# A hybrid decoder layer on one core: later due times for the values that come back from DRAM, and the gates' products in two parts

## The chip, the cores and the metric

The kernel runs on one core of a Trainium2 chip. The metric is the device time of one execution in microseconds (us), as the median of several runs; less is better. The engines that matter are TensorE (PE in the profile, with its weight loads apart as PEld), ScalarE (ACT), VectorE (DVE), GpSimd (POOL) and SyncE (SP), whose queue issues the DMAs.

## The reference: what is computed

One inference step of a decoder layer with width 2048, for 256 tokens of a new sequence and 8 × 8 tokens of running ones: 320 tokens in all, in float32.

```python
proj = jnp.einsum('btd,de->bte', x, w_in)
(ml_q, ml_k, ml_v, ml_i, ml_f, ml_o, hg_q, hg_f, hg_i, hg_g, gate_a, gate_b) = jnp.split(proj, offs, axis=-1)
...
ig = (ml_i + b_ig).transpose(0, 2, 1)
lf = jax.nn.log_sigmoid(ml_f + b_fg).transpose(0, 2, 1)
h, C, n, m = _mlstm(q, k, v, ig, lf, C0, n0, m0)       # 4 heads, key width 256, value width 512
...
o, S = _hgrn2(hq, jnp.log(f), 1.0 - f, hi, S0)         # 8 heads, key width 128, value width 256
...
merged = jax.nn.sigmoid(gate_a) * ya + jax.nn.sigmoid(gate_b) * yb
x1 = _layernorm(DEEPNORM_ALPHA * x + merged @ w_out, ln1_g, ln1_b)
y  = _layernorm(DEEPNORM_ALPHA * x1 + relu(x1 @ w_up)**2 @ w_down, ln2_g, ln2_b)
```

The outputs are y and the new states C, n, m and S of both groups of tokens. `ml_i` and `ml_f` are eight columns only, the input and forget gates of the four mLSTM heads; everything that decays in these heads is worked out from them.

## The kernel before, in words

**Tiles and units.** The weights of all the big products are cut into 304 tiles of 128 columns, in the order of `TILES`: for each of the four mLSTM heads four tiles of values (`mv`), two of keys (`mk`), two of queries (`mq`) and two of the merge gates; then for each of the eight HGRN heads merge gates, `hf`, `hq` and two `hi`; then the output gates, the branch projections, `w_out`, and the feed-forward part. A tile is sixteen steps over k, each with 128 rows of the weight and all 320 tokens. Each step is three matmuls, since a float32 number is held as a high and a low half: xh·wh, xl·wh and xh·wl. All of them are line 340, as the helper `mm` issues them. The first three tiles are interleaved over k, because x and the weights are still arriving (x comes in chunks of `FIRST_K`: one k at a time to 10, then two at a time).

**Weights.** Half a tile is a unit, 128×1024 floats, 512 KB. It is loaded into one of three raw buffers (`wr<-wt`), ScalarE writes its high half (`wh<-wr`, line 334, called from `prep`), VectorE the low half (`wl<-wr,wh`, line 504, in `low_half`), and then the load of the third unit after it is issued (`reload`). Hence the two splitting engines have a unit of weights to do every 24 matmuls, and do all else between.

**The order of the work** comes from a planner that runs while the program is written (`Sched`, lines 145 to 240). It keeps a clock for every engine, `s.t`. The main loop, `run_main`, writes the matmuls of a step, adds 147 ns each to the clock of PE, and then calls `pump`. That lets chains (generators, by priority) put their own next instructions on the engines, where the planner's times allow it: a request `("act", cost, fn)` is written at once if it would be ready soon; `wait(e)` holds the chain until the planned time `e.t`; `acq` and `rel` take and give buffers and banks. Each engine runs its instructions in the order written; semaphores keep the data right. So a planned time moves no data: it decides behind what an instruction stands in its engine's queue.

**What the change touches.**

- `gates`, line 762, is called by `run_main` ahead of step (0, 10), that is, tile 0, k = 10. It multiplies the sixteen chunks of x with the eight gate columns (in all sixteen products of 32 output rows, four row strips side by side in one bank), adds 2500 ns to PE's clock, and starts two chains. `rows` (line 798) copies the bank, sums the strips (two products with the constant `sel`, `bank<-f,cst`), and makes everything that decays: Abs, Exp and Ln on ScalarE, the rest on VectorE; its results are stored to DRAM (`scr<-f`) and each head reads its rows of it back, broadcast to all partitions (`f2a<-scr`, in `m_E`). `lb` (line 772) does the bounds of the HGRN gates.
- `m_V`, line 973. The values of an mLSTM head are transposed by 32×32 blocks on VectorE and stored to DRAM in four DMAs (`rows_to`, `vtD<-f`); `rows_from` (line 1014) reads them back as 128×1024 (`ra<-vtD`), waits in the plan for 5000 ns after the issue, and then splits them: ScalarE `ra<-ra` 128×1024 (line 334), VectorE `ra<-ra` (line 1808, in `split`).
- `h_i`, line 1571, the same for the values of an HGRN head (`sD`, `f2r<-sD`, 128×512).

**What stands around it.** In each mLSTM head `m_KW` (line 1077) multiplies the keys with the decay (line 1087), transposes them by blocks (line 1097), splits them (lines 334 and 1100), sums them (lines 1109 to 1111), and stacks the halves of the sample tokens' keys: `f<-f2a` on ScalarE and line 1058 on VectorE, followed by two transposes on TensorE (line 1122). This happens twice, so there are two pairs of transposes in a head. `m_CP` stores keys (`kD<-ra`), `turned` (lines 1303 to 1325) stores the heads' outputs (`hT<-f`, with its own transposes, line 1320, and copies `f<-bank` of 128×64).

**Queues.** All these DMAs, and the weights', are issued by SP in the order written (line 343); the profile calls that SPq.

Of the kernel before, what the change touches and what calls it, by code (L numbers as in the profile page):

```python
# [21 lines left out]
KT = 16  # L22
# [212 lines left out]
def wait(*evs):  # L235
    return ("wait", evs)


def acq(pool, n=1):
    return ("acq", pool, n)  # L240


def rel(pool, item):
    return ("rel", pool, item)


def post(ev):
    return ("set", ev)
# [47 lines left out]
class Program:  # L296
# [216 lines left out]
    def run_main(self):  # L513
        s = self.s
        todo, step = {}, []
        for n, (i, k) in enumerate(STEPS):
            t = TILES[i]
            u = i + FIRST * (k // 8) if i < FIRST else 2 * i + k // 8
            if n == 0:
                self.first()  # L520
            elif (i, k) == (0, 10):
                self.gates()
            if k == 0:
                self.before(i, t)
                pool = self.sbank if i == FIRST - 1 else self.mbank
                s.until(lambda: pool.free)
                pool.free.sort(key=lambda x: x[0])
                at, b = pool.free.pop(0)
                mh, ml, evs = self.moving(t)
                todo[i] = pool, b, b[:, :mh.shape[2]], mh, ml, evs  # L530
                s.t["pe"] = max(s.t["pe"], at)
                if t[0] == "up":
                    self.up_old[t[1:3]] = self.old[0]
            pool, b, o, mh, ml, evs = todo[i]
            if t[0] == "up" and not self.old[k]:
                o, mh, ml = b[:, :TOK], self.xh, self.xl
                s.t["pe"] = max(s.t["pe"], self.u_at[k])
            if i < FIRST:
                s.t["pe"] = max(s.t["pe"], self.x_at[k])
            while self.prep(u not in self.unit):  # L540
                pass
            assert u in self.unit, (u, self.next_prep)
            (hi, lo), at = self.unit[u]
            if evs is not None:
                s.until(lambda: evs[k].t is not None)
                at = max(at, evs[k].t + LAT)
            kk = slice(128 * (k % 8), 128 * (k % 8) + 128)
            step.append((i, t, u, b, o, hi[:, kk], lo[:, kk], mh, ml))
            if i < FIRST - 1:
                continue  # L550

            s.t["pe"] = max(s.t["pe"], at)
            for n in range(3):
                if i < FIRST and k == KT - 1:
                    break
                for _, _, _, _, o, wh, wl, mh, ml in step:
                    self.mm(o, wl if n == 2 else wh, (ml if n == 1 else mh)[:, k, :], start=n + k == 0, stop=n == 2 and k == KT - 1)
                s.t["pe"] += 147.0 * len(step)
                if n < 2 and i < FIRST:
                    s.pump(s.t["pe"])  # L560
            if t[0] == "up" and self.want[k] is not None:
                self.want[k].t, self.want[k] = s.t["pe"], None
            for i, t, u, b, o, wh, wl, mh, ml in step:
                if i < FIRST and k == KT - 1:
                    for n in range(3):
                        self.mm(o, wl if n == 2 else wh, (ml if n == 1 else mh)[:, k, :], start=False, stop=n == 2)
                    s.t["pe"] += 441.0
                if k % 8 == 7:
                    self.give(u)
                if k == KT - 1:  # L570
                    del todo[i]
                    s.spawn(self.evac(t, b), 0)
                if i < FIRST - 1:
                    s.pump(s.t["pe"])
            step = []
            s.pump(s.t["pe"])
        self.carve_o()
        self.main_end.t = s.t["pe"]
        s.until(lambda: not s.chains)
# [179 lines left out]
        for x, name, sl in ((self.n0_in, "n0", np.s_[:]), (self.lmask, "lmask", np.s_[:])):  # L759
            yield ("sp", 620, lambda: self.dma(x, d[name][sl]))  # L760

    def gates(self):

        s, b = self.s, self.gbank
        for k in range(KT):
            x = k % 4
            self.mm(b[32 * x:32 * x + 32, :TOK], self.gw[:, k, :], self.xs[:, k, :], start=k < 4, stop=k >= KT - 4)
        s.t["pe"] += 2500.0
        s.spawn(self.rows(b), 1)
        s.spawn(self.lb(), 2)  # L770

    def lb(self):

# [199 lines left out]
    def m_V(self, h):  # L973
        m = self.mh[h]
        if h:
            yield wait(self.mh[h - 1]["Vt"])
        yield wait(*m["v"])
        vr = m["vr"]
        yield from self.rows_to(vr[:, 0:1024], self.vtD[h])
        yield wait(m["Vs"])  # L980
        yield rel(self.vr, vr)
        vhl = yield acq(self.vhl)
        m["vhl"] = vhl
        yield from self.rows_from(self.vtD[h], vhl[:, 0], vhl[:, 1])
        yield post(m["Vt"])

    def m_Vs(self, h):
# [23 lines left out]
        e.t = t + 5000.0  # L1011
        yield wait(e)

    def rows_from(self, of, hi, lo):

        x = lo.bitcast(F32)
        t = yield ("sp", 620, lambda: self.dma(x.rearrange("p (n k) -> p n k", k=128), of.rearrange("j (i p) k -> p (j i) k", p=128)))
        e = Ev()
        e.t = t + 5000.0
        yield wait(e)  # L1020
        yield from self.split(x, hi, lo, hi.shape[1])

# [548 lines left out]
    def h_i(self, h):  # L1571
        m = self.hh[h]
        if h:
            yield wait(self.hh[h - 1]["I"])
        yield wait(*m["i"])
        yield self.mdone()
        yield from self.rows_to(m["iv"][:, 0:512], self.sD[h])
        it = yield acq(self.it)
        m["it"] = it
        yield from self.rows_from(self.sD[h], *it)  # L1580
        yield post(m["I"])

    def h_vs(self, h):
# [656 lines left out]
```

## Time and profile before

| | us |
|---|---|
| median of three runs | 2285.47 |
| lowest, highest | 2284.47, 2285.81 |
| the profiled execution | 2287.0 |
| its span in the profile | 2285.2 |

The mean granted clock of TensorE in the profiled execution is 0.998. In the profile's groups a line such as `L334 ACT ACTIVATE wh<-wr 128x1024 ... x431` is one kind of instruction: line 334 of the kernel, on ScalarE, from tile `wr` to tile `wh`, 431 times. In the timeline a row gives start, duration, engine, line, operation, tiles and shapes, how many of them in a row, and in brackets how long the engine had been idle ahead of it and what ended this idle time. A matmul's duration (0.31 us) is its time through the array; a new one starts every 0.147 us.

### The profile page before, as it was taken

Reading aid. Unit: us, or ns where it says so; the run is one execution under the profiler, and the core shown is the slowest. Engines: PE = TensorE matmul, PEld = TensorE weight load, DVE = VectorE, ACT = ScalarE, POOL = GpSimd, SP = SyncE. Lnnn points to the kernel's source line nnn. Section 1 sums busy time; section 2 is a strip of 40 time slices with the busy share of each in tenths; the row PEclk is TensorE's granted clock in tenths of the full one; section 3 lists DMA queues with packets and bytes.
Section 4 is the critical chain, followed back from the end, with each engine's and each line's share of the span. In section 5 each row is a group of like instructions: output and inputs, shape, how many; then the busy total and the mean of one; then the engine's idle time right before and its main releaser. Section 6 shows DMA issues by size and latency. Waiting matters only on the chain.

```text
span 2285.2 us, 39088 instructions
## 1 busy us (share of the span) xinstructions
PE 2270.6 (99%) x15546; PEld 2232.6 (98%) x15546; DVE 1422.2 (62%) x2490; ACT 1010.8 (44%) x1574; POOL 12.3 (1%) x42
## 2 busy tenths in 40 slices
PE   9999999999999999999999999999999999999998
PEld 9989899999999999999999999999999999999998
DVE  6667667888888876555555769444444444444555
ACT  5444445555555565444433447433433343334434
POOL 0000000000000000000000000000000000000000
PEclk9999999999999999999999999999999999999999
DMA  7898886666677655544555644444444444444555
GB/s 240 322 292 281 295 270 224 205 221 208 212 226 233 204 180 178 175 171 172 175 174 191 205 157 148 152 153 148 148 150 154 148 148 151 153 148 148 193 185 185
DMA packets 253536, 441.28 MB, mean 193 GB/s; under 512 B 106908, under 2 KB 149028, under 8 KB 252328
## 3 DMA queue, kind: packets, MB, share of 16 engines
q1 hardware_dynamic: 250664, 432.48, 56.8%
q0 software_dynamic: 2688, 6.29, 0.9%
q8 instruction: 122, 2.00, 0.4%
q14 instruction: 62, 0.51, 0.1%
HBM read 380.45 MB, written 58.24 MB: 192 GB/s over the span
## 4 chain that ended last, share of the span: by engine, by line
PE 92%; DMA 3%; DVE 1%; ACT 1%; SPq 1%; issue 0%; ACTq 0%; DVEq 0%
PE bank L340 92%; DMA wr<-wt 1%; SPq L343 1%; DVE wl L504 1%; DMA ra<-vtD 0%; ACT f3m L334 0%; ACT wh L334 0%; DMA f<-xT 0%; DMA f2a<-scr 0%; DMA scr<-f 0%; DMA hT<-f 0%; DMA rx<-wt 0%; ACT oC L334 0%; ACT f L334 0%; ACT ra L334 0%
## 5 line engine op out<-in xcount | busy, mean ns | idle before, releaser
L340 PE MATMUL bank<-xh,wh 128*128 128x320 f32 x2408 | 759.7, 317 | 0.0
L340 PE MATMUL bank<-xh,wl 128*128 128x320 f32 x2408 | 743.9, 310 | 0.8 <-DVE wl L504 0.8
L340 PE MATMUL bank<-xl,wh 128*128 128x320 f32 x2408 | 740.9, 309 | 0.0
L334 ACT ACTIVATE wh<-wr 128x1024 fp32r<-128x1024 f32 (+1 forms) x431 | 452.3, 1049 | 614.1 <-PE bank L340 575.8
L504 DVE TENSOR_TENSOR wl<-wr,wh 128x1024 fp32r<-128x1024 f32 x423 | 516.6, 1221 | 304.3 <-ACT wh L334 301.6
L340 PEld LDWEIGHTS bank<-xh,wh 128*128 128x128 f32 x2408 | 453.1, 188 | 6.4 <-issue 3.9
L340 PEld LDWEIGHTS bank<-xl,wh 128*128 128x128 f32 x2408 | 453.1, 188 | 2.6
L340 PEld LDWEIGHTS bank<-xh,wl 128*128 128x128 f32 x2408 | 453.5, 189 | 1.3 <-DVE wl L504 1.3
L334 ACT ACTIVATE bb<-wr 128x1024 fp32r<-128x1024 f32 x179 | 189.6, 1060 | 356.0 <-PE bank L340 342.3
L504 DVE TENSOR_TENSOR bb<-wr,bb 128x1024 fp32r<-128x1024 f32 x179 | 219.0, 1224 | 163.1 <-ACT bb L334 163.1
L340 PE MATMUL bank<-xh,bb 128*128 128x320 f32 (+1 forms) x1280 | 284.1, 309 | 0.0
L340 PE MATMUL bank<-ra,bb 128*128 128x320 f32 x1264 | 283.3, 308 | 0.0
L340 PE MATMUL bank<-rxb,bb 128*128 128x320 f32 x1112 | 255.0, 309 | 0.0
L340 PE MATMUL bank<-ra,wh 128*128 128x320 f32 x892 | 248.8, 308 | 0.0
L340 PEld LDWEIGHTS bank<-xh,bb 128*128 128x128 f32 x1280 | 214.6, 188 | 0.0
L340 PEld LDWEIGHTS bank<-ra,bb 128*128 128x128 f32 x1264 | 210.6, 188 | 0.2
L340 PE MATMUL bank<-xl,bb 128*128 128x320 f32 (+1 forms) x640 | 197.5, 309 | 0.0
L340 PEld LDWEIGHTS bank<-rxb,bb 128*128 128x128 f32 x1112 | 188.4, 188 | 0.2
L340 PE MATMUL bank<-rxb,wl 128*128 128x320 f32 x596 | 183.7, 308 | 0.0
L340 PE MATMUL bank<-rxb,wh 128*128 128x320 f32 x596 | 183.7, 308 | 0.0
L340 PEld LDWEIGHTS bank<-ra,wh 128*128 128x128 f32 x892 | 161.4, 188 | 0.0
L340 PEld LDWEIGHTS bank<-xl,bb 128*128 128x128 f32 x640 | 120.2, 188 | 0.0
(325 smaller groups left out, 2132.9 us busy)
## 6 DMA issues: line engine op xcount, KB each, us to landing
wr<-wt SPq DMA_DIRECT2D x602, 512.0 KB
rx<-C SPq DMA_DIRECT2D x34, 256.0 KB
Cs<-rx SPq DMA_DIRECT2D x34, 256.0 KB
f<-C SPq DMA_DIRECT2D x30, 256.0 KB
Cs<-f SPq DMA_DIRECT2D x30, 256.0 KB
f<-xT SPq DMA_DIRECT2D x26, 160.0 KB
vD<-ra SPq DMA_DIRECT2D x4, 1024.0 KB
f<-S SPq DMA_DIRECT2D x8, 512.0 KB
```

The source lines that it names most:

```text
L334: return self.nc.scalar.activation(out, in_, func, **kw)
L340: self.nc.tensor.matmul(*a, **kw)
L343: self.nc.sync.dma_start(out, in_)
L504: self.V().tensor_tensor(lo, raw, hi.bitcast(F32), ALU.subtract)
```

## The change

The gates' products are written in two parts, k = 0 to 11 ahead of step (0, 10) and k = 12 to 15 ahead of step (0, 12), and cost the plan 78 ns each (1248 in all) and not 2500; `rows` and `lb` start behind the second part. The wait between the issue of a readback and its split is 10000 ns for the mLSTM values and 7000 ns for the HGRN values, where both had 5000. Each engine gets as many instructions as before; the order in which they are written is another. From line 772 on the changed kernel's lines have a number one higher (the split is line 1809, the transposes 1123).

```diff
-            elif (i, k) == (0, 10):
-                self.gates()
+            elif i == 0 and k in (10, 12):
+                self.gates(*((0, 12) if k == 10 else (12, KT)))
...
-    def gates(self):
+    def gates(self, k0, k1):
...
-        for k in range(KT):
+        for k in range(k0, k1):
             x = k % 4
             self.mm(b[32 * x:32 * x + 32, :TOK], self.gw[:, k, :], self.xs[:, k, :], start=k < 4, stop=k >= KT - 4)
-        s.t["pe"] += 2500.0
-        s.spawn(self.rows(b), 1)
-        s.spawn(self.lb(), 2)
+        s.t["pe"] += 78.0 * (k1 - k0)
+        if k1 == KT:
+            s.spawn(self.rows(b), 1)
+            s.spawn(self.lb(), 2)
...
-        yield from self.rows_from(self.vtD[h], vhl[:, 0], vhl[:, 1])
+        yield from self.rows_from(self.vtD[h], vhl[:, 0], vhl[:, 1], 10000.0)
...
-    def rows_from(self, of, hi, lo):
+    def rows_from(self, of, hi, lo, ahead):
...
-        e.t = t + 5000.0
+        e.t = t + ahead
...
-        yield from self.rows_from(self.sD[h], *it)
+        yield from self.rows_from(self.sD[h], *it, 7000.0)
```

## The prediction

> **What bounds the kernel now.** I read the page first, then the waits of TensorE, then the timeline of each engine at every wait found.
>
> ```profile
> PE 2270.6 (99%) x15546; PEld 2232.6 (98%) x15546; DVE 1422.2 (62%) x2490; ACT 1010.8 (44%) x1574; POOL 12.3 (1%) x42
> ...
> PE 92%; DMA 3%; DVE 1%; ACT 1%; SPq 1%; issue 0%; ACTq 0%; DVEq 0%
> ...
> 824.78 1436.54 PE bank L340 x9787
> ...
> PE bank L1122 <- DVE f2a L1058: 2.5, 1, 2.5
> PE bank L1122 <- DVE f L1058: 1.9, 1, 1.9
> PE bank L340 <- POOL ones L666: 1.0, 1, 1.0
> PE bank L340 <- DVE wl L504: 0.8, 2, 0.5
> PE bank L340 <- DMA f<-xT: 0.6, 1, 0.6
> PE bank L340 <- ACT f2r L334: 0.4, 1, 0.4
> ```
>
> TensorE is busy for 99% of the span. The chain's long piece gives 1436.54 / 9787 = 0.147 us per matmul, and no number of matmuls changes. So all that the change can win is the waits. Without the first one, of POOL, which it doesn't touch, they are 2.5 + 1.9 + 0.8 + 0.6 + 0.4 = 6.2 us. The 1.9 us one was followed by slow matmuls:
>
> ```profile
> 233.13 0.31 PE L340 MATMUL bank<-xh,wl 128*128 128x320 f32 x1
> 235.38 0.33 PE L1122 MATMUL bank<-cst,f 128*128 128x128 f32 x1 [1.95 <-DVE f L1058]
> ...
> 236.53 0.62 PE L340 MATMUL bank<-xh,wh 128*128 128x320 f32 x1
> ...
> 239.61 0.41 PE L340 MATMUL bank<-xh,wl 128*128 128x320 f32 x1
> ...
> 200.00:300.00 100.00, 98.05 (x663) 92.79 (x662) 70.28 (x141) 43.92 (x83) 0.00 (x0) 0.98 0.88 282
> ```
>
> From 236.53 to 239.61 eleven matmuls take 0.28 us each where 0.147 is usual: 1.5 us more, in the one stretch of 100 us whose granted clock is 0.98 and not 1.00. The ceiling of the gain is thus about 6.2 + 1.5, with some 0.2 us of slow restart after each wait near 9 us: 0.4% of the span. I call 0.2% (4.57 us) the least that a measurement of this kernel tells from no change.
>
> The sum below is made against the profiled run, 2287.0 us with a span of 2285.2. It is 1.5 us above the median of the runs, 2285.47, so I take 1.5 off at the end. Shifts are those of TensorE after against before; plus is later.
>
> **1. The gates' products in two parts.**
>
> ```profile
> 19.18 1.52 PE L340 MATMUL bank<-f 128*32 128x320 f32 x16
> 21.25 0.73 PE L340 MATMUL bank<-f 128*32 128x320 f32 x4 [0.55 <-DMA f<-xT]
> ...
> 28.29 1.04 ACT L334 ACTIVATE wh<-wr 128x1024 fp32r<-128x1024 f32 x1
> 29.90 0.47 ACT L334 ACTIVATE f<-f 4x320 f32<-4x320 f32 x1 [0.57 <-DVE f L823]
> 30.96 1.39 ACT L334 ACTIVATE f<-bank 128x256 f32<-128x256 f32 x6 [0.59 <-PE bank L340]
> ...
> 31.65 0.31 PE L340 MATMUL bank<-xh,wh 128*128 128x320 f32 x1
> ```
>
> The 0.55 us wait for the last chunk of x goes: its transfer lands while 18 other matmuls (2.6 us) run. Against it stands a second change from full to 32-row products and back. No row prices one alone: the rows leave 21.25 to 31.65 without a gap that could be it, so I bound it by 0 and by two pitches, 0.3, and take 0.15, between ends that are near each other. Gain 0.4.
>
> But the chain of the gates (ScalarE's Abs and Exp, two weight splits between them) starts 18 matmuls later too. Those pieces now fall at 30 to 31.5 us, right ahead of the six copies that empty the first three tiles' banks. Before, the copies start at 30.96, take 0.23 each, and the fourth tile's first matmul follows at 31.65. In the changed order one 1.04 us split and one 0.47 us step come just before them, and bank 0's second copy is the fourth and not the second of the six: 2 × 0.23 = 0.46, and of the 1.5 us ahead I count a third, since ScalarE sat idle for 0.59 and 0.57 there. Shift at 32 us: about +0.9, the gain above included; from −0.4 (all hidden) to +1.4.
>
> **2. Head 0.** There the readback's halves move 39 matmuls back.
>
> ```profile
> 60.37 0.35 DVE L928 TENSOR_SCALAR f<-f2a,misc 128x256 f32<-128x256 f32 x1 [3.87 <-DMA f2a<-scr]
> ...
> 61.72 1.23 DVE L1808 TENSOR_TENSOR ra<-ra 128x1024 fp32r<-128x1024 f32 x1
> ...
> 63.67 1.22 DVE L504 TENSOR_TENSOR wl<-wr,wh 128x1024 fp32r<-128x1024 f32 x1
> ...
> 64.95 0.42 PE L340 MATMUL bank<-xh,wl 128*128 128x320 f32 x1 [0.28 <-DVE wl L504]
> ...
> 70.32 0.33 PE L1122 MATMUL bank<-cst,f 128*128 128x128 f32 x1
> ```
>
> The gates' rows come back from DRAM at 60.3; their chain begins 2.6 us later and may regain 0.7 to 1.5 of that where ScalarE stood idle (0.57, 0.59), so I take 61.4 to 62.2. The weights' low half (63.67) no longer has the readback's 1.23 us in front of it, so it ends near where it did. From the rows to the transposes (70.32) it was 10.0 us; without the readback's 1.23 in between, of which I count 0.5 to 1, it is 9 to 9.5: transposes at 70.9 to 71.7 with the nearer ends paired. Shift: +1.0 (+0.2 to +1.8), no longer hidden by anything: VectorE's chain is what ends last here.
>
> **3. Head 1, the longest wait.**
>
> ```profile
> 147.87 1.06 ACT L334 ACTIVATE ra<-ra 128x1024 fp32r<-128x1024 f32 x1 [3.59 <-DMA ra<-vtD]
> 148.83 0.42 ACT L334 ACTIVATE f<-bank 128x320 f32<-128x320 f32 x1
> ...
> 152.80 1.06 ACT L334 ACTIVATE wh<-wr 128x1024 fp32r<-128x1024 f32 x1 [2.10 <-DMA wr<-wt]
> 153.76 0.29 ACT L334 ACTIVATE f<-f2a 128x128 fp32r<-128x128 f32 x1
> ...
> 148.96 1.23 DVE L1808 TENSOR_TENSOR ra<-ra 128x1024 fp32r<-128x1024 f32 x1 [2.74 <-ACT ra L334]
> ...
> 155.03 0.28 DVE L1058 TENSOR_TENSOR f<-f2a,f 128x128 fp32r<-128x128 f32 x1
> ...
> 152.28 0.33 PE L1122 MATMUL bank<-cst,f2a 128*128 128x128 f32 x1 [2.54 <-DVE f2a L1058]
> ...
> 156.09 0.27 PE L1122 MATMUL bank<-cst,f 128*128 128x128 f32 x1
> ...
> 147.88 0.44 SPq L343 DMA_DIRECT2D wr<-wt  x1
> ```
>
> Before, the halves wait until 147.87 for the readback, and the key's small pieces queue behind them on ScalarE and VectorE: so the first transposes wait 2.54 us. The change puts the halves 36 and 39 matmuls back, behind those pieces; the first transposes are then ready at about 149.3, and this wait goes.
>
> What is late next is the second pair, 24 matmuls on (156.09). In the new order its piece f<-f2a stands on ScalarE behind a weight split and then the readback's half, and on VectorE behind L504 and L1808. The weight split waits for wr, which SP issues at 147.88, at its place in a queue that the change does not reorder up to there; so it still starts at 152.80. Then 153.86 + 1.06 = 154.9 for the half, + 1.23 = 156.2 for L1808, + 0.28 and a start for L1058: transposes at about 156.5. TensorE, there by 153.3, waits 3.2 us. Shift behind it: +0.4 by these absolute times, up to +1.4 if SP carries the +1.0 of head 0; −2.1 if the weights land 2.5 us sooner. Taken: +0.7. The wait moves by 4 us and is not shorter.
>
> A page speaks for the change: the Trainium skill, "DMA: Bandwidth & Descriptors", section "Rules for kernel authors", has it that a DMA is issued early and its semaphore awaited late, so that its fixed cost lies beside work. By that rule alone the 2.54 us go; the rows agree for the first pair, and 152.80 speaks against it for the second.
>
> **4. Heads 2 and 3.**
>
> ```profile
> 231.74 1.06 ACT L334 ACTIVATE ra<-ra 128x1024 fp32r<-128x1024 f32 x1 [3.46 <-DMA ra<-vtD]
> ...
> 233.64 0.22 ACT L334 ACTIVATE f<-bank 128x64 f32<-128x64 f32 x1 [0.41 <-DMA hT<-f]
> ...
> 234.71 0.30 ACT L334 ACTIVATE f<-f2a 128x128 fp32r<-128x128 f32 x1
> ...
> 315.78 1.06 ACT L334 ACTIVATE ra<-ra 128x1024 fp32r<-128x1024 f32 x1 [4.08 <-DMA ra<-vtD]
> ...
> 319.75 0.42 PE L340 MATMUL bank<-xh,wl 128*128 128x320 f32 x1 [0.50 <-DVE wl L504]
> ```
>
> Head 2: the half no longer stands before f<-f2a, but the copies f<-bank still do, and one of them waits for a store hT to land at 233.6. Behind it come 0.22 + 0.42 + 0.30 on ScalarE and 0.28 on VectorE: transposes at 234.8, not 235.38. That is −0.6; but the second pair, 36 matmuls on, now has the half and one weight split in front of it on both engines, and I count +0.6 there (one 1.06 us piece that isn't quite covered). The bounds of head 2 are −3.5 (wait and slow matmuls go) and +2.3 (half and split halves, 1.06 + 1.23, uncovered). Head 3: the half goes 30 matmuls back, and the wl that was 0.50 late is ready before it is asked: −0.5, from −0.7 to +0.5.
>
> On the 1.5 us of slow matmuls: the Trainium skill, "TensorE: Matmul & The Clock Gate", section "What's actually happening", says that the clock is halved after about one idle window of 3.4 us, free-running. This trace has it after 1.95 us and not after 2.54; by the page it is chance, and the 3.2 us of head 1 would cost by my estimate up to half a window, 1.7 us. I leave the 1.5 in both.
>
> **5. The HGRN heads.** The wait of 7 us moves the 128x512 halves 12 to 45 matmuls back in five heads; in three they come 12 to 42 earlier, as the planner has shifted what lies around them. In the new order 18 to 78 matmuls (2.6 us and more) stand between each and its first reader. The one wait there (0.4) may go or move: 0, from −0.5 to +1.5. From 824.78 on the chain is TensorE alone, and the order is the same.
>
> **Queues.** No engine gets an instruction more. SP keeps the order of the vtD stores, readbacks and weight loads in heads 0 and 1; in head 2 one hT store, whose copy waits for the landing at 233.6 or the one before it, comes ahead of a weight load. That load goes out some 3 us later, but it is for the third unit after the one at hand (a unit is 24 matmuls, 24 × 0.147 = 3.5 us), so I cost it at nothing. POOL's order is untouched.
>
> **Sum.** +0.7 after head 1; −0.6 and +0.6 in head 2; −0.5 in head 3; 0 in the HGRN heads: +0.2, so about 2287.2 profiled, **2285.7** as a median.
>
> **Rivals.**
> - **A, the waits really go.** Weights land in time in head 1 and the stores in head 2: 2.5 + 1.9 + 0.5 + 0.6 (gates), 1.5 of slow matmuls, less 1.0 to 2.0 of head 0: −5 to −6, 2279.5 to 2280.5. For it: the first pair is free by 149.3. Against it: the waits of 2.10 for wr and 0.41 for hT, which have nothing to do with the halves. This is also what the rule of awaiting late gives.
> - **B, slower: the late half blocks the second pair in every head.** Each loses 1.06 + 1.23 = 2.3 us where TensorE was on time before. It decides where the half is issued behind a weight split whose transfer lands less than 3.5 us before the pair is due. Three heads, less the first pair's gain in head 1, plus the 1.0 of head 0: 3 × 2.3 − 2.5 + 1.0 = +5.4, and +6.9 with 1.5 of slow matmuls in a second place: 2290.9 to 2292.4. For it: head 1 above. Against it: in head 2 the half stands 30 matmuls (4.4 us) ahead of the pair that it could block.
> - **C, it does nothing to the time:** the halves are issued later, but wait for the same landings (147.87, 231.74, 315.78 on ScalarE): ±0.5 us.
>
> **How the numbers follow.** Forecast, waits that move: 0.45, within 0.2%. A: 0.25, nearly all faster by over 0.2%. B: 0.25, slower by over 0.2%. C: 0.05, within. So faster 0.25, same 0.50, slower 0.25. The range leaves out about the far half of A and of B: 2280 to 2291.5.
>
> **What would show it.** Right: no wait at 149 us, one of about 3 us before an L1122 at 153 to 157; ScalarE's `wh` near 152.8 still waiting for wr; the fourth tile's start at 32.3 to 32.8; transposes of head 0 at 71. Wrong: TensorE without a wait of over 1 us between 100 and 330 (A), or three of over 2 us (B); or another granted clock in a stretch after 330 us.

## The result, and the profile after

| | before | after |
|---|---|---|
| median of 18 runs each, us | 2287.99 | 2291.31 |
| lowest, highest, us | 2284.47, 2289.63 | 2283.78, 2294.97 |
| span of the profiled execution, us | 2285.2 | 2289.5 |

The ratio is 1.0015, with a 95% interval from 1.0009 to 1.0021: 2 to 5 us slower, 3.4 in the middle. It is less than the 0.2% that the prediction called the least that can be told from no change; with eighteen runs of each it can just be told. The forecast time, 2285.7, was reckoned from three runs of the kernel before with a median of 2285.47; in these eighteen it takes 2287.99. So 2.5 of the 5.6 us between 2285.7 and 2291.31 are not the change's. The time lies just inside the forecast range, 2280 to 2291.5.

The waits of TensorE in the profile after (what was waited for, us in total, times, longest):

```profile
PE bank L1123 <- DVE f L1059: 8.6, 3, 3.3
PE bank L340 <- ACT f L334: 1.0, 1, 1.0
PE bank L340 <- POOL ones L666: 1.0, 1, 1.0
PE bank L1123 <- DVE f2a L1059: 0.9, 1, 0.9
```

Without POOL's they are 8.6 + 1.0 + 0.9 = 10.5 us, where before they were 6.2. The difference, 4.3, is that of the two spans (2289.5 − 2285.2 = 4.3). Of the old waits that the change could touch one is left, that of the first pair of transposes in head 2 (1.95 us at 235.38 before, 2.69 at 237.38 now). The others are gone, and there are four new ones. In the timeline (start, duration, engine, line; in brackets the idle time and what ended it):

```profile
32.16 0.41 PE L340 MATMUL bank<-xh,wh 128*128 128x320 f32 x1 [1.01 <-ACT f L334]
...
156.63 0.33 PE L1123 MATMUL bank<-cst,f 128*128 128x128 f32 x1 [3.33 <-DVE f L1059]
...
237.38 0.33 PE L1123 MATMUL bank<-cst,f 128*128 128x128 f32 x1 [2.69 <-DVE f L1059]
...
321.08 0.33 PE L1123 MATMUL bank<-cst,f2a 128*128 128x128 f32 x1 [0.88 <-DVE f2a L1059]
...
328.94 0.33 PE L1123 MATMUL bank<-cst,f 128*128 128x128 f32 x1 [2.55 <-DVE f L1059]
```

The longest is the one that the prediction gave for head 1 (156.5, 3.2 us). The queue of ScalarE and then of VectorE there, in the timeline of the changed kernel:

```profile
152.92 1.06 ACT L334 ACTIVATE wh<-wr 128x1024 fp32r<-128x1024 f32 x1 [5.63 <-DMA wr<-wt]
153.88 1.04 ACT L334 ACTIVATE ra<-ra 128x1024 fp32r<-128x1024 f32 x1
154.83 0.29 ACT L334 ACTIVATE f<-f2a 128x128 fp32r<-128x128 f32 x1
...
154.01 1.23 DVE L504 TENSOR_TENSOR wl<-wr,wh 128x1024 fp32r<-128x1024 f32 x1 [5.46 <-ACT wh L334]
155.15 1.22 DVE L1809 TENSOR_TENSOR ra<-ra 128x1024 fp32r<-128x1024 f32 x1
156.29 0.29 DVE L1059 TENSOR_TENSOR f<-f2a,f 128x128 fp32r<-128x128 f32 x1
```

ScalarE stood idle for 5.63 us because the weights at the head of its queue had not landed. Behind them came the values' half, and only then the small piece f<-f2a that the transposes need. On ScalarE that order costs nothing here: f<-f2a is done at 155.12, while VectorE is at the weights' low half (L504) until 155.2. What counts is VectorE, where the half L1809 takes 1.22 us between L504 and L1059. From the start of the weights' split to the transposes it is 156.63 − 152.92 = 3.7 us, of which TensorE is covered for 0.4. The half's own data was there long before (in the kernel before, its readback had landed by 147.87); by these rows it could have been done in those 5.63 us, or behind the small piece.

One caution before the experiments. A single profile does not say which part of the change costs what: kernels with the same order of instructions differ by several us (below), so the parts are told apart by ratios over many runs, and the profiles only show where the waits stand.

### The profile page after: what moved, and what is told of

Same layout as the page of the kernel before. It is cut to its first block, busy times and chain, and to the rows that moved or that the text cites. A ratio compares the mean times of both kernels' runs of the same rounds, so it can differ in the third digit from the quotient of the medians.

```text
span 2289.5 us, 39080 instructions
## 1 busy us (share of the span) xinstructions
PE 2270.9 (99%) x15546; PEld 2232.3 (97%) x15546; DVE 1421.9 (62%) x2490; ACT 1009.2 (44%) x1574; POOL 12.4 (1%) x42
## 4 chain that ended last, share of the span: by engine, by line
PE 96%; DMA 2%; ACT 1%; DVE 1%; SPq 0%; issue 0%; ACTq 0%; POOL 0%; POOLq 0%
PE bank L340 95%; DMA wr<-wt 1%; ACT wh L334 1%; DVE wl L504 0%; ACT f3m L334 0%; DMA hT<-f 0%; SPq L343 0%; ACT f L334 0%; ACT oC L334 0%; ACT ra L334 0%; PE bank L1123 0%; PE bank L1041 0%; PE bank L1321 0%; ACT f2l L334 0%; DVE ra L1809 0%
## 5 line engine op out<-in xcount | busy, mean ns | idle before, releaser
L504 DVE TENSOR_TENSOR wl<-wr,wh 128x1024 fp32r<-128x1024 f32 x423 | 517.1, 1223 | 312.3 <-ACT wh L334 304.2
L504 DVE TENSOR_TENSOR bb<-wr,bb 128x1024 fp32r<-128x1024 f32 x179 | 219.2, 1225 | 164.4 <-ACT bb L334 164.3
```

What stands on the lines that cost most here:

```text
L504: self.V().tensor_tensor(lo, raw, hi.bitcast(F32), ALU.subtract)
```

## The experiments

The theory: the two halves moved behind other pieces, and these pieces (the second pair of transposes in head 1, the stores hT in head 2, weights in head 3) are now late instead. So the place of the half in the queues of ScalarE and VectorE decides, and the gates' products and the HGRN wait have little to do with it. The rivals: that the gates' chain, started 18 matmuls later, costs the time; that the HGRN wait does; or that all waits are only those for weights that SP sends late.

The ratios, each with its 95% interval, against runs of the kernel before on the same chip:

| kernel | ratio | interval |
|---|---|---|
| the change | 1.0015 | 1.0009 to 1.0021 |
| the change, again (e5_after) | 1.0013 | 1.0004 to 1.0022 |
| gates in two parts alone (e1_gates) | 1.0002 | 0.9993 to 1.0010 |
| mLSTM wait of 10000 alone (e2_values) | 1.0008 | 0.9999 to 1.0017 |
| the same again (e10_values_again) | 1.0013 | 1.0003 to 1.0022 |
| HGRN wait of 7000 alone (e3_hgrn) | 1.0007 | 0.9998 to 1.0017 |
| the same again (e11_hgrn_again) | 1.0004 | 0.9995 to 1.0013 |
| change, half behind both pairs (e4_behind) | 0.9998 | 0.9989 to 1.0007 |
| change, six buffers for hT (e6_tails) | 0.9999 | 0.9989 to 1.0009 |
| change, both of these (e7_behind_tails) | 0.9978 | 0.9970 to 0.9987 |
| change, wide hT stores on POOL (e9_pool_stores) | 0.9995 | 0.9986 to 1.0003 |
| before, six buffers for hT (e12_before_tails) | 1.0003 | 0.9994 to 1.0012 |
| before, half behind and six buffers (e13_before_behind_tails) | 0.9974 | 0.9965 to 0.9984 |

**The gates' products alone.** From the changed kernel, both waits are set back:

```diff
-        yield from self.rows_from(self.vtD[h], vhl[:, 0], vhl[:, 1], 10000.0)
+        yield from self.rows_from(self.vtD[h], vhl[:, 0], vhl[:, 1], 5000.0)
...
-        yield from self.rows_from(self.sD[h], *it, 7000.0)
+        yield from self.rows_from(self.sD[h], *it, 5000.0)
```

> The gates' products in two parts alone, all readbacks split after 5000 as before. Theory (the moved halves carry the loss): the wait of 0.55 us for the last chunk of x goes, one of about 1.0 us for the copies of the first tiles' banks comes near 31 us, the waits at 149, 233 and 319 us stay as before; time within 2 us of before (ratio 0.9992 to 1.0008). Rival (the chain of the gates, started later, carries it): 3 to 4 us slower than before, with a longer wait ahead of the transposes of head 0 near 70 us.

Measured 1.0002. The new wait is there, and the one for the last chunk of x is gone. In the timeline of this kernel:

```profile
32.75 0.41 PE L340 MATMUL bank<-xh,wh 128*128 128x320 f32 x1 [1.02 <-ACT f L334]
...
154.81 0.47 PE L1123 MATMUL bank<-cst,f2a 128*128 128x128 f32 x1 [3.25 <-DVE f2a L1059]
```

So 0.55 us of waiting for x was given up for 1.02 of waiting for a bank. The first pair of head 1 waits as it did before, and longer (there 2.54 us). This profile also has a wait of 0.92 ahead of head 0's transposes, as the rival had it; the ratio leaves the rival's 3 to 4 us out.

**The mLSTM wait alone, twice.** Gates in one part, the HGRN wait at 5000.

```diff
-        yield from self.rows_from(self.vtD[h], vhl[:, 0], vhl[:, 1])
+        yield from self.rows_from(self.vtD[h], vhl[:, 0], vhl[:, 1], 10000.0)
```

> The mLSTM values' wait of 10000 alone, gates in one part, HGRN wait 5000. Theory: this part has the loss, 2.5 to 5 us slower than before; no wait at 149 us, a wait of 3 to 3.5 us ahead of the second pair of transposes of head 1 (153 to 157 us), one of about 2.5 us near 237 and one of about 2.5 us near 329. Rival (gates or HGRN carry it): within 1.5 us of before.

> The mLSTM values' wait of 10000 alone once more, to narrow its interval (1.0008, from 0.9999 to 1.0017). Theory (it carries most of the loss): 1.0005 to 1.0018, the waits near 156, 237 and 328 us again. Rival (the loss is the sum of three small parts): 1.0000 to 1.0005.

1.0008 and 1.0013: 2 to 3 us, most of the loss, though the first of the intervals still holds 1. The 1.8 us of the first are less than the 2.5 to 5 that were expected. The waits stand where the theory put them; the one near 329 was 1.22 us, where about 2.5 was expected. In the second execution the first two are about a third shorter and the third is longer. The timeline of TensorE in the first of the two, then in the repeat:

```profile
156.13 0.48 PE L1122 MATMUL bank<-cst,f 128*128 128x128 f32 x1 [2.88 <-DVE f L1058]
...
236.87 0.33 PE L1122 MATMUL bank<-cst,f 128*128 128x128 f32 x1 [2.96 <-DVE f L1058]
...
327.36 0.33 PE L1122 MATMUL bank<-cst,f 128*128 128x128 f32 x1 [1.22 <-DVE f L1058]
```

```profile
155.52 0.33 PE L1122 MATMUL bank<-cst,f 128*128 128x128 f32 x1 [1.87 <-DVE f L1058]
...
233.88 0.33 PE L1122 MATMUL bank<-cst,f 128*128 128x128 f32 x1 [1.87 <-DVE f L1058]
...
323.53 0.33 PE L1122 MATMUL bank<-cst,f 128*128 128x128 f32 x1 [1.94 <-DVE f L1058]
```

**The HGRN wait alone, twice.** Gates in one part, the mLSTM wait at 5000; only `h_i` has its new one:

```diff
-        yield from self.rows_from(self.sD[h], *it)
+        yield from self.rows_from(self.sD[h], *it, 7000.0)
```

> The HGRN values' wait of 7000 alone. Theory: the halves have 2.6 us and more to their first readers, so within 1 us of before; the one wait of 0.4 us near 548 may go. Rival (late halves in eight heads add up): 2 to 4 us slower, with new waits of TensorE between 440 and 800 us.

> The HGRN values' wait of 7000 alone once more (1.0007, from 0.9998 to 1.0017). Up to 411 us its order is that of before, and behind that its profile lost nothing more than before's. Theory (it costs nothing, the first reading was scatter of the first 400 us): 0.9995 to 1.0005. Rival (it carries part of the loss): 1.0005 to 1.0015, with new waits of TensorE between 440 and 800 us.

1.0007, then 1.0004: both hold 1, and neither of the two readings in the expectation is settled by the ratios; the second interval leaves up to 3 us. The span of the first is 2289.8, of the second 2282.2, with the same program. Up to about 411 us its order is that of the kernel before, and the first wait of head 1 alone reads so in the two executions:

```profile
152.97 0.48 PE L1122 MATMUL bank<-cst,f2a 128*128 128x128 f32 x1 [2.62 <-DVE f2a L1058]
```

```profile
151.04 0.33 PE L1122 MATMUL bank<-cst,f2a 128*128 128x128 f32 x1 [1.56 <-DVE f2a L1058]
```

(The first fence is the first run's timeline, the second the repeat's.) Nearly all of the difference of 7.6 us between the spans arises ahead of 411 us: at the 2340th matmul the first is 4.63 us behind the profile of before, the repeat 2.75 ahead; at the end 4.59 and 3.07. Behind 411 us neither lost more than before; there are no new waits over 0.2 us there, and the one of 0.42 us at 548.71 of the kernel before is gone. That speaks for the HGRN wait costing nothing: what is ahead of 411 us it can't have caused.

**The half behind both pairs.** The changed kernel; `m_V` waits in the plan also for the event that is posted when both pairs of transposes of its head have been written.

```diff
-        yield from self.rows_from(self.vtD[h], vhl[:, 0], vhl[:, 1], 10000.0)
+        yield from self.rows_from(self.vtD[h], vhl[:, 0], vhl[:, 1], 10000.0, m["KS"])
...
-    def rows_from(self, of, hi, lo, ahead):
+    def rows_from(self, of, hi, lo, ahead, *also):
...
-        yield wait(e)
+        yield wait(e, *also)
```

> The changed kernel, with the mLSTM values split only when the second pair of transposes of the same head has been written (the half then stands behind both pairs in every head). Theory (the second pair waits for the half ahead of it on ScalarE and VectorE, 1.06 and 1.23 us, and for the weights ahead of that): the wait near 153 to 157 us falls from 3.3 to about 1.0 to 2.2 us, the one near 329 us loses less than 1.2, since there the half is done before the weights land; 1 to 3 us faster than the changed kernel. Rival (only the late weights matter, the half costs nothing): these waits stay within 0.3 us of 3.3 and 2.5, and the time that of the changed kernel.

0.9998: by the middles of the two intervals, which do not touch, about 4 us faster than the changed kernel (1.0015), where 1 to 3 was expected. Here is the same place of head 1, ScalarE first, then VectorE and TensorE:

```profile
152.98 1.06 ACT L334 ACTIVATE wh<-wr 128x1024 fp32r<-128x1024 f32 x1 [3.54 <-DMA wr<-wt]
153.94 0.29 ACT L334 ACTIVATE f<-f2a 128x128 fp32r<-128x128 f32 x1
...
154.07 1.23 DVE L504 TENSOR_TENSOR wl<-wr,wh 128x1024 fp32r<-128x1024 f32 x1 [3.37 <-ACT wh L334]
155.21 0.28 DVE L1059 TENSOR_TENSOR f<-f2a,f 128x128 fp32r<-128x128 f32 x1
...
155.55 0.33 PE L1123 MATMUL bank<-cst,f 128*128 128x128 f32 x1 [1.20 <-DVE f L1059]
...
237.28 0.47 PE L1123 MATMUL bank<-cst,f 128*128 128x128 f32 x1 [3.58 <-DVE f L1059]
```

The split of the weights starts at the same time as in the changed kernel (152.98 against 152.92), and L1059 now follows L504 directly, at 155.21 and not at 156.29. The transposes come 1.1 us sooner: so much of the 3.33 us is the half's, and the other 2.2 are the weights'. The wait is not 2.2 but 1.20 us because TensorE gets to the pair 1.05 us later (155.55 − 1.20 = 154.35, against 156.63 − 3.33 = 153.30). It has waited 1.13 us at the first pair of this head, at 149.05, which the planner now writes 15 matmuls sooner (the second pair 8 sooner). In head 3 the waits are gone altogether, which the expectation did not have: it gave the wait at 329 to the weights. What the half has to do with those weights is shown with the stores on POOL's queue, below. Head 2 still waits, and its cause is the next experiment.

**More buffers for the head outputs.** In head 2 ScalarE's queue looks like this in the changed kernel:

```profile
234.92 0.22 ACT L334 ACTIVATE f<-bank 128x64 f32<-128x64 f32 x1 [5.24 <-DMA hT<-f]
236.25 0.55 ACT L334 ACTIVATE f<-bank 128x64 f32<-128x64 f32 x2 [1.11 <-DMA hT<-f]
236.69 0.31 ACT L334 ACTIVATE f<-f2a 128x128 fp32r<-128x128 f32 x1
```

The copies of 128x64 have two buffers between them, and each waits until the store of the one before the last has landed, 5.24 us at first. Six buffers in place of two (free room in another tile):

```diff
-        self.tail = Pool([B(64) for _ in range(2)])
+        self.tail = Pool([B(64) for _ in range(2)] + [self.f2[:, 2640 + 64 * i:2704 + 64 * i] for i in range(4)])
```

> The changed kernel with six buffers and not two for the 128x64 pieces of the head outputs, so that ScalarE's copies f<-bank no longer wait for a store hT to land. Theory (in head 2 the landing of hT, ahead of the key's piece in ScalarE's queue, makes TensorE's wait of 2.7 us near 237): that wait falls below 1.2 us, the one near 157 stays; 1 to 3 us faster than the changed kernel. Rival (something else is late there, such as the split of the weights): the wait near 237 stays above 2 us.

> The kernel before with six buffers and not two for the 128x64 pieces of the head outputs. There the copies f<-bank stand behind the values' half, which waits for its readback. Theory (before, each wait is one for the readback at the head of ScalarE's queue, and buffers for hT alone do not free it): the wait near 149 to 152 stays at 2 us or more, the one near 235 falls from 1.95 to about 1; within 0.1% of before. Rival (landings of hT are the cause in both kernels): 0.9980 to 0.9990 of before.

In the changed kernel: 0.9999, against 1.0013 for the change in the same set of runs (its own waits there, below); the two intervals overlap a little, from 1.0004 to 1.0009. The wait of head 2 is gone, those of heads 1 and 3 stay:

> The changed kernel itself once more, as the yardstick for the runs beside it. Theory: 1.0009 to 1.0021 of before again; of its waits, the one of 3.3 us near 157 (weights, then half, ahead of the second pair) and the one near 237 (store hT) come at the same places, each within 1 us.

```profile
156.44 0.33 PE L1123 MATMUL bank<-cst,f 128*128 128x128 f32 x1 [2.75 <-DVE f L1059]
...
237.11 0.33 PE L1123 MATMUL bank<-cst,f 128*128 128x128 f32 x1 [4.18 <-DVE f L1059]
...
330.52 0.48 PE L1123 MATMUL bank<-cst,f 128*128 128x128 f32 x1 [3.19 <-DVE f L1059]
```

```profile
156.75 0.33 PE L1123 MATMUL bank<-cst,f 128*128 128x128 f32 x1 [2.05 <-DVE f L1059]
...
324.95 0.33 PE L1123 MATMUL bank<-cst,f 128*128 128x128 f32 x1 [2.49 <-DVE f L1059]
```

(First the change again, then the change with six buffers; between 200 and 300 us the second has no wait of TensorE at all. The expectation that the repeat's waits would lie within 1 us of the first profile's did not hold at 237: 4.18 against 2.69.)

In the kernel before, six buffers do nothing that can be measured: 1.0003 (its order on TensorE is another from head 2 on). Its wait at 235 is 2.16 us, where about 1 was expected. There the half stands ahead of the copies f<-bank and waits for its own readback, so freeing the copies frees little:

```profile
231.34 1.06 ACT L334 ACTIVATE ra<-ra 128x1024 fp32r<-128x1024 f32 x1 [3.24 <-DMA ra<-vtD]
232.30 0.54 ACT L334 ACTIVATE f<-bank 128x64 f32<-128x64 f32 x2
```

**Both together**, on the changed kernel and on the kernel before (there with gates and HGRN wait as they were):

> Both: six buffers for those pieces, and the values split only behind the second pair of transposes. Theory: the waits of TensorE between 100 and 400 us add up to less than 4 us (9.5 in the changed kernel); 3 to 6 us faster than the changed kernel, 1 to 3 us faster than before. Rival (taking a wait away only moves it to the next late transfer): sum of the waits there above 6 us, time within 1.5 us of the one with the half behind alone.

> The kernel before with six buffers for those pieces and the values split only behind the second pair of transposes; gates in one part and the HGRN wait at 5000, as before. Theory (place of the half and the buffers do it all, the gates and the HGRN wait nothing): 0.9970 to 0.9985 of before, TensorE's waits between 100 and 400 us below 3 us in sum. Rival (the split gates or the HGRN wait of the changed kernel have a part in the 0.9978): 0.9985 to 0.9995.

0.9978 and 0.9974, about 5 and 6 us faster than before, and the first about 8 us faster than the change in the same set of runs (1.0013), where 3 to 6 was expected. What TensorE still waits for between 100 and 400 us is 1.14 + 0.95 and 1.21 + 0.76 us; of the second kernel:

```profile
148.12 0.33 PE L1122 MATMUL bank<-cst,f2a 128*128 128x128 f32 x1 [1.21 <-DVE f2a L1058]
...
154.18 0.33 PE L1122 MATMUL bank<-cst,f 128*128 128x128 f32 x1 [0.76 <-DVE f L1058]
```

and a table of stretches (busy time and number of PE, PEld, DVE, ACT, POOL; granted clock, share of the DMA engines, GB/s):

```profile
200.00:300.00 100.00, 100.00 (x687) 94.84 (x686) 71.82 (x139) 44.61 (x85) 0.00 (x0) 1.00 0.89 287
300.00:400.00 100.00, 100.00 (x687) 94.86 (x686) 69.60 (x133) 49.06 (x82) 1.42 (x8) 1.00 0.78 246
```

TensorE is busy throughout from 200 to 400 us, at a clock of 1.00. Its waits, without POOL's, are 0.40 for x and the two above, 2.4 us in all, and the span of 2279.4 less these is 2277.0. For the kernel before it is 2285.2 − 6.2 − 1.5 (slow matmuls) = 2277.5, and for the change 2289.5 − 10.5 − 1.5 = 2277.5. So what sets these three apart is the waits of TensorE and the slow matmuls behind them. The intervals of the two overlap: with half and buffers in place, the split gates, the HGRN wait and the 10000 in place of 5000 add nothing that can be measured. The runs also lie closer together: 2280.4 to 2282.8 us for e13_before_behind_tails (9 runs), where the kernel before beside it spread from 2283.2 to 2293.2 (31 runs).

**The wide hT stores on POOL's queue.** The changed kernel, with the eight 32x16x32 stores of `turned` issued by GpSimd:

```diff
-                yield ("sp", 620, lambda: self.dma(
+                yield ("pool", 1000, lambda: self.nc.gpsimd.dma_start(
```

> The changed kernel with the 32x16x32 stores hT issued by GpSimd's queue and not by SP's. Theory (SP is behind in heads 1 to 3, so weights land late): the weight load that went out at 146.8 us goes out 2 to 5 us sooner, the split near 152.9 starts before 151, and the wait of 3.3 us near 157 falls below 2 us; 1 to 4 us faster than the changed kernel. Rival (the DMA engines are full, share 0.88, and SP's place in time doesn't matter): the split stays at 152 or later and the wait at 3 us.

0.9995, about 4 us faster than the change. But in head 1, where its theory was to be tested, the step did not come out. The weight load went out at 144.28, 2.5 us sooner, and its split still began at 152.35; in the timeline of SP, then ScalarE, then TensorE:

```profile
144.28 0.85 SPq L343 DMA_DIRECT2D wr<-wt  x1
...
152.35 1.06 ACT L334 ACTIVATE wh<-wr 128x1024 fp32r<-128x1024 f32 x1 [0.30 <-DMA wr<-wt]
...
151.66 0.33 PE L1123 MATMUL bank<-cst,f2a 128*128 128x128 f32 x1 [1.48 <-DVE f2a L1059]
```

The split waited only 0.30 us there, for here the half stood ahead of it and had waited for its readback; but the weights themselves landed no sooner than 152.35, 8.1 us after their issue, against 6.2 in the changed kernel (146.75 to 152.92). That much is as the rival had it. The second pair of head 1 does not wait, the first does (1.48 us), and all waits between 100 and 400 us are 5.5 us in sum, against 9.5 in the changed kernel.

In head 3 the theory does come out. SP, ScalarE and TensorE there, in the changed kernel and then with the stores on POOL's queue:

```profile
317.11 0.92 SPq L343 DMA_DIRECT2D hT<-f  x2
...
318.70 2.01 SPq L343 DMA_DIRECT2D hT<-f  x2
320.81 1.12 SPq L343 DMA_DIRECT2D wr<-wt  x2
...
326.37 1.06 ACT L334 ACTIVATE wh<-wr 128x1024 fp32r<-128x1024 f32 x1 [2.87 <-DMA wr<-wt]
```

```profile
314.76 3.48 SPq L343 DMA_DIRECT2D wr<-wt  x2
...
320.93 1.06 ACT L334 ACTIVATE wh<-wr 128x1024 fp32r<-128x1024 f32 x1 [0.58 <-DMA wr<-wt]
...
324.10 0.27 PE L1123 MATMUL bank<-cst,f 128*128 128x128 f32 x1
```

Both splits are of the same unit of weights, both come behind the values' half, and each starts 5.6 to 6.2 us after its load was issued. With four stores hT and a readback ahead of it in SP's queue the load goes out at 320.81, and the transposes wait 2.55 us; without the stores it goes out at 314.76, and they wait for nothing. In the kernel before and in the one with the half behind both pairs these four stores are not at that place either (the load went out at 312.99 and 317.85). So in head 3 it is the order on SP that makes the wait, and not the half itself; the order came with the later due time, for in both runs with the mLSTM wait alone the four stores stand there too.

## Why the prediction came out as it did

Forecast was a time within 0.2% of before, by waits that move and do not shrink, with a sum of +0.2 us. The time is inside, at +0.15%, but the sum is not what happened: the waits moved and also grew, from 6.2 to 10.5 us. The profiles differ by +4.3 us and the runs, by their ratio, by about +3.4. That this stayed within 0.2%, and within the range by 0.2 us, is partly luck. Counted by matmuls, TensorE is behind the profile of before by about 2.2 us after head 1 (forecast 0.7), 1.7 after head 2 (0.7), 4.7 after head 3 (0.2) and 4.4 at the end. Head 1's excess is the slow matmuls, 1.5 us, which in the kernel before came in head 2; the forecast had left them in both, and there is one such stretch in both. The step that failed most is head 3. Point by point:

- **Gates.** The wait for x went, as said. The copies came late as said: TensorE's fourth tile starts at 32.16 (forecast 32.3 to 32.8), +0.5 us and not +0.9. e1_gates puts the whole part at 1.0002.
- **Head 0.** Forecast +1.0, measured −0.2: the transposes are at 70.11 and not at 70.9 to 71.7. The rows came back at 60.9, 0.5 later than before, where 1.1 to 1.9 was assumed. The step from there (9 to 9.5 us) came out as 70.11 − 60.87 = 9.2, but not for the reason given: the half (L1809, at 66.65 for 1.22 us) still stands between the two. (With 9 to 9.5 the forecast should also have read 70.4 to 71.7; 70.9 to 71.7 adds 9.5 at both ends.) The term mis-sized is how much of the 2.6 us the chain regains.
- **Head 1.** Right in its times: weights at 152.92 (152.80 forecast), half, L1809, then the transposes at 156.63 (156.5), after a wait of 3.33 (3.2). Only L1809 follows L504 on VectorE, and not ScalarE's half as the forecast added it up; the two end about 0.3 us apart. The slow matmuls behind it also came (below).
- **Head 2.** Forecast 234.8, measured 237.38. The step that failed is that the landing of hT stayed at 233.6. The two stores that the copies wait for went out at 230.15 and 231.58, where the kernel before had them at 227.49 and 228.89, and the second landed at 236.2. TensorE was 2.2 us later there, and the copies and their stores came later with it. The pair is also asked for 6 matmuls (0.9 us) sooner in TensorE's order. e6_tails shows that this landing makes the wait. The second pair, for which +0.6 was counted, did not wait.
- **Head 3.** Forecast −0.5 with no new wait; measured 0.88 and 2.55 us of new waits. ScalarE had done the half by 323.5 and then waited 2.87 us for weights at 326.37, whose load stood behind four stores hT in SP's queue. The failed step is under "Queues": it went through SP's order in heads 0 to 2 only, put what it found in head 2 at nothing, and gave head 3 no term for it. e9_pool_stores, with the half in the same place and these stores in another queue, has no wait at this pair.
- **HGRN.** Forecast 0; 1.0007 and 1.0004, both with 1 inside, and nothing lost behind 411 us in either profile.
- **Rivals.** A, that the waits really go, failed in this change and is true of e7_behind_tails and e13_before_behind_tails, where the half stands behind both pairs and not between them. B, three heads with 2.3 us each, was right in its count: three waits of over 2 us, the sign that the prediction named for it. But only in head 1 does the half hold up the pair, and there it costs 1.1 and not 2.3 us; +5.4 to +6.9 us is more than the +3.4 measured. C was wrong: one wait of six is left where it was, and the interval of 1.0015 does not hold 1.

What stays open: how much of the loss is the gates' and how much the HGRN wait's (their intervals reach from −0.07% to +0.10% and from −0.05% to +0.17%), why the weights of head 1 land at about 152.5 whether they are sent for at 144.3 or at 146.8, and what the half behind both pairs gives in the kernel before without the buffers, which was not run.

## What to carry to other kernels

A later due time in a planner moves an instruction behind the next ones in its engine's queue: read in the profile which piece the critical engine needs next there, and put the late one behind that, not merely later. In head 1, 10000 ns put the half just ahead of the second pair of transposes; tied to the event that the pair has been written, it made the kernel 0.17% faster than that, and 0.35% with four small buffers more. Buffers paid only where they were what the head of the queue waited for: in the kernel before they gave nothing, behind the moved half 0.2%. And a new due time reorders every queue, that of the DMAs too: the wait of head 3 came from there, though the change names no transfer but the readbacks.

## What the runs showed of the hardware

Slow matmuls follow idle time of TensorE, but not each time. The traces keep the granted clock, and in them it is 1.00 or 0.50 and nothing else. Away from the ends of the program each stretch at 0.50 lasts 3.41 us, or twice that, and the stretches at 1.00 between them are whole multiples of 3.41 us (23, 24, 26 and 49). So the clock is set anew every 3.41 us. Here are such windows of the changed kernel, three around its wait in head 1 and two around that in head 2 (the first number behind the comma is TensorE's busy time, the granted clock is third from the end):

```profile
154.12:157.53 3.41, 0.90 (x7) 0.88 (x7) 3.34 (x8) 2.27 (x4) 0.00 (x0) 1.00 0.53 178
157.53:160.95 3.42, 3.42 (x15) 3.29 (x14) 0.97 (x1) 0.73 (x2) 0.00 (x0) 0.50 1.00 267
160.95:164.36 3.41, 3.41 (x29) 1.61 (x28) 1.56 (x2) 0.92 (x1) 0.00 (x0) 1.00 1.06 389
232.63:236.04 3.41, 2.06 (x15) 1.79 (x13) 0.00 (x0) 0.22 (x1) 0.00 (x0) 1.00 0.89 279
236.04:239.45 3.41, 2.07 (x15) 2.05 (x16) 1.52 (x2) 1.81 (x5) 0.00 (x0) 1.00 0.66 211
```

Of the wait in head 1, 2.5 us fall into one window, and the next runs at half the clock: matmuls start about 0.27 us apart there, where 0.147 is usual. The wait of 2.69 us in head 2 is cut by the edge of a window into 1.35 and 1.34, and nothing follows. With the fourteen traces cut in this way, between 20 and 900 us, all eleven windows of full clock with 1.95 us or more of idle time are followed by a slow one. Of those with 1.83 us or less two are, both with 1.51 us in more than one wait (e3_hgrn and e12_before_tails, near 320 us). A slow window with 0.7 to 1.1 us of idle time of its own was followed by a second one, four times. In the kernel before the wait of 1.95 us lay in one window and that of 2.54 was cut into 1.33 and 1.21: hence slow matmuls after the shorter and none after the longer. A wait thus costs its own length and, if about 1.9 us of one window are idle, some 1.5 us more; where it lies over the windows decides. The Trainium skill, "TensorE: Matmul & The Clock Gate", section "What's actually happening", has a free-running window of 3.4 us and half the clock after at least one idle window. The window's length and the half are as here; a window that was idle for 1.95 of its 3.41 us was enough.
